# The rest of a split weight by an accumulating DMA in place of a VectorE subtraction

## Chip, core and metric

The kernel runs on one core of one Trainium2 chip. The metric is the device time of one execution in microseconds, as the median of several runs. The core has TensorE (PE in the profile, with its weight loads as PEld), VectorE (DVE), ScalarE (ACT), GpSimd (POOL) and SyncE (SP), and 16 DMA engines, which work through the queues of the engines that issue DMAs. Operands lie in SBUF, the results of matmuls in PSUM, inputs and outputs in DRAM.

## What is computed

Four layers of a diffusion backbone over 256 latent tokens and 256 context tokens, 2048 features wide. The mixers are Fourier, mLSTM in both directions, attention, and Fourier again (on the latent tokens alone).

```python
for i in range(DEPTH):                       # 4
    kind = i % N_MIXERS                      # Fourier, mLSTM, attention
    shift, scale, gate = jnp.split(sc @ ada_w[i] + ada_b[i], 3, axis=-1)
    hx = _rmsnorm(x, norm_g[i]) * (1.0 + scale[:, None]) + shift[:, None]
    # hc: the same for the context
    # kind 0: y = (fourier_mix(h) * silu(h @ w_gate)) @ w_out
    # kind 1: q, k, v, o, g, z = split(h @ w_in); y = (norm(sigmoid(o) * mlstm) * silu(z)) @ w_out
    # kind 2: q, k, v, z = split(h @ w_in);       y = (attention * silu(z)) @ w_out
    x = x + gate[:, None] * y_x
    if ctx_out:
        ctx = ctx + gate_c * y_c
return _rmsnorm(x, final_g)
```

All inputs are float32. What matters here are the products with the large weights: w_gate and w_out of both Fourier layers, w_in and w_out of the other two.

## The kernel before

A product of full precision is made from three products of the rounded type float32r. Each operand is split into a rounded part and a rest: activations h and l, weights wh and wl. TensorE adds h·wh, h·wl and l·wh in PSUM (L296 and L307).

The weights of all products are one stream of tiles of two k-tiles, [128, 2, 512], that is 512 KB each. `groups` (L250) gives the order of the matrices, 50 groups of 512 columns with 8 tiles each, so 400 tiles. One tile is called a weight step below. `make_w` (L256) makes one: a DMA on SP's queue brings it into `raw` (named wraw in the profile, 4 buffers, `WRAW`), ScalarE rounds it into `wh` (L265), VectorE subtracts that from `raw` into `wl` (L266). `wh` and `wl` have 3 buffers each (`WHL`). `next_w` (L269) hands the next pair to a product, in the order in which they are made.

`gemm` (L274) is one group: for each pair of k-tiles it takes a pair of weights and lets every accumulating bank take its three products. With 512 tokens (both streams) a weight step is 24 matmuls with 512 columns. In the attention layer's later part and in layer 3 there are the latent tokens alone, and a step is half of that.

Other work is woven into the products in pieces (`Weave`, L89): the mixers' own work, and the adaLN modulation of later layers. The latter reads its weights (`araw`, 512 KB at a time) by DMAs on SP's queue too (L175 for TensorE's variant, L198 for VectorE's), and VectorE multiplies and adds them up at L206. Along the path of TensorE also stand, for the profile's rows, the normalized operand's rest `l` (L405 in the modulation), the query and key norm (L1006), the sums of squares (L463) and the new residual `rn` (L456).

The order of TensorE's instructions is that of the program (L42). The instructions of each other engine, DMA issues on SP's and POOL's queue included, are put in order by a scheduler when the kernel is built, and each engine and each queue then works in that order, with a wait in front of an instruction whose operands or buffer are not there yet. GpSimd has little to do: in the mLSTM core it makes masks from `ub`, which a DMA brings (L779), and clears a block of `eb` (L802).

Of the kernel before, what the change touches and what calls it, by code (L numbers as in the profile page):

```python
# [21 lines left out]
# buffers of adaLN weights, weights, their parts  # L22
ARAW, WRAW, WHL = 3, 4, 3
# adaLN chunks of layer 1 on the tensor engine; pieces of woven work per piece of a product
# [3 lines left out]
# columns of the packed constants  # L28
# [17 lines left out]
def _build(tc, nc, top, A, out):  # L46
# [42 lines left out]
    class Weave:  # L89
        """Generators run in turn, each step a piece of work."""  # L90
# [35 lines left out]
    class Lazy:  # L126
        """Parts of an operand's k-tiles, made when they are first asked for."""
# [9 lines left out]
        def half(self, kt, s):  # L137
            """One stream's part."""
            self.have[kt] = self.make(kt, s, self.have.get(kt))

    def ahead(gen):
        """A product up to where all of its operand is made."""
        for what in gen:
            if what == "made":
                return gen

    def after(key, made):
        """An operand of which the last four k-tiles come from woven work."""
        def get(kt):
            if kt >= 12:  # L150
                fill.finish(key)
            return made[kt]
        return Lazy(get)
# [6 lines left out]
    def ada_finish(l, s, kts, src, nv):  # L160
        """src: the products by vector and k-tile."""
        v0 = 2 - nv
        dst = ada[:, l, s, v0:2, kts]
        V.tensor_tensor(dst, src, adab[:, l, s, v0:2, kts], ALU.add)
        if s == SC:
            V.tensor_tensor(dst, dst, ng[:, l, v0:2, kts], ALU.mult)

    def ada_pe(l, s, c, place):
        """256 columns of a layer's modulation for both vectors: on the tensor engine, k-tiles in
        turn on four column groups."""  # L170
        ps = bank()
        for kq in range(4):
            pp, tag, bufs = next(place[0])
            raw = pp.tile([P, 2, 512], F32, tag=tag, name="araw", bufs=bufs)
            Q.dma_start(raw, A["ada_p"][l, s * 8 + c, kq])  # L175
            rv = raw.rearrange("p a b -> p (a b)").rearrange("p (q n) -> p q n", q=4)
            for q in range(4):
                T.matmul(ps[32 * q:32 * q + 32, :256], cpad[:, 4 * kq + q, :], rv[:, q, :],  # L178
                         start=kq == 0, stop=kq == 3)
            yield 1  # L180
        r = ap_.tile([P, 256], F32, tag="ar", name="ar", bufs=1)
        S.copy(r, ps[:, :256])
        yield 1
        pt = bank()
        for i in range(2):
            T.transpose(pt[:, 128 * i:128 * i + 128], r[:, 128 * i:128 * i + 128], ident)
        m = ap_.tile([P, 2, 4], F32, tag="am", name="am", bufs=4)[:, :, 0:2]
        V.tensor_reduce(m, pt[:, :256].rearrange("p (i q c) -> p c i q", i=2, q=4)[:, 0:2], AX.X, ALU.add)
        ada_finish(l, s, slice(2 * c, 2 * c + 2), m, 2)
        yield 1  # L190

    def ada_dve(l, s, j, nv, row=None):
        """The same on the vector engine; with `row`, added to all partitions' rows there."""
# [32 lines left out]
    def ada_chain(chunks):  # L226
        """ada_dve in turn; each one's last part on the tensor engine comes three steps late, when
        the vector engine has it."""
# [27 lines left out]
    def make_w():  # L256
        """Two k-tiles of a group's weights, as rounded part and rest."""
# [8 lines left out]
        V.tensor_tensor(wl, raw, wh.bitcast(F32), ALU.subtract)  # L266
# [7 lines left out]
    def gemm(hl, orient, t0, t1, done, first=False, used=None, halves=False, begin=None):  # L274
        """One group of 512 weight columns, in pieces; `done(b, psum)` takes each bank.
        orient A: bank b has columns 128b.. on partitions, tokens t0..t1 free.
        orient B: bank b has tokens t0 + 128b.. on partitions, columns free.
        halves (A): each stream in banks of its own, the last k-tiles for the context first;
        done(b, psum, stream).
        begin: the first four k-tiles for the context first; begin(k) has work after its k-th."""  # L280
# [7 lines left out]
        def one(b, kt, w2, s=None):  # L288
# [7 lines left out]
            for ip, (x, w) in enumerate(((h, wh), (h, wl), (l, wh))):  # L296
# [3 lines left out]
                else:  # L300
                    lhsT, rhs, o = w[:, 128 * b:128 * b + 128], x[:, c], banks[b][:, c.start - t0:c.stop - t0]
                    # a bank's second part comes into the group that its first has begun
# [71 lines left out]
    def rstd_cols(pp, acc, tiles, name, wait=lambda: None):  # L374
        """rstd by token on partitions, [P, tiles]; acc: squares summed over all k-tiles but the last,
        and those of the last. `wait` has work for the tensor engine meanwhile."""
# [12 lines left out]
    def rstd_rows(pp, r, nt):  # L389
        """The same along the free dimension, on all partitions, in PSUM."""  # L390
# [7 lines left out]
    def modulate(l, kt, src, rows, pp, s, have):  # L398
        """hT of one k-tile and stream as parts, in `have` if those are there; src, rows: its tokens."""
# [9 lines left out]
    class Norm:  # L409
        """The norm between two layers with both streams, one after the other: the squares' sums come  # L410
        with the last product of the one, the modulation with the first of the other."""
# [24 lines left out]
    def out_proj(pp, px, l, hl, old, new_dram, c0, rates, tag="xf", bufs=5, gate=None, norm=None):  # L436
        """R = R_old + gate * (y @ W); rows of R on chip, their squares' sum, R to DRAM."""
# [3 lines left out]
        for g in range(4):  # L441
# [27 lines left out]
            if g < 3 or norm is None:  # L469
                if g == 3:  # L470
                    # the table with the square root, ahead of its use
# [18 lines left out]
    def fourier(pp, l, j, eo, F, s0):  # L490
        """eo [P, 2 (sum, difference), seqs, 512]: tokens t +- (t + 128), normed, not yet scaled by
        the modulation. F [P, 4, seqs * 256] receives the mixed group, transposed."""
# [32 lines left out]
        for par in range(2):  # L525
            for m in range(2):
                ps = bank()
                # columns: cosines of tokens 0, 2, .., 128, 1, 3, .., 127; sines of even and odd ones
# [26 lines left out]
    # =====================================================================  # L555
    # layer 0: Fourier
    # =====================================================================
    with ExitStack() as st:
# [17 lines left out]
        for l in range(4):  # L576
            # scale: norm_g * (1 + bias + product)
# [14 lines left out]
        with ExitStack() as st2:  # L592
# [3 lines left out]
            def turned(k2):  # L596
                """hT of two k-tiles, then the first product's part with the two before."""
# [70 lines left out]
    # =====================================================================  # L668
    # layer 1: mLSTM, both directions, positions in the order context, latent
    # =====================================================================  # L670
# [14 lines left out]
    with ExitStack() as st:  # L685
# [10 lines left out]
        def gates():  # L696
            """Rows of the 32 gates: input gates on partitions 0.. (forward) and 32.. (backward), forget
            gates on 64.. and 96.. ."""
# [3 lines left out]
            # k-tiles in turn on four column groups, then their sums on the rows they belong to  # L702
# [31 lines left out]
            # backward rows with each stream in its flipped order  # L734
# [33 lines left out]
        def core(c):  # L768
            """The pair's two heads, in pieces: scores (A), transposed weights (B), sums of values (C)."""
            def load(hh):  # L770
                h = 2 * c.p + hh
                ub, um = [], []
                for d in range(2):
                    u = p1.tile([P, 512], F32, tag="ub", name=f"ub{d}", bufs=2)
                    Q.dma_start(u, rows_u[d, h:h + 1, :].to_broadcast([P, 512]))
                    # the blocks on the diagonal, where a token sees a part of them
# [151 lines left out]
        def load_y(kt):  # L928
            """An earlier pair's y, once the last product has used the k-tile."""
# [41 lines left out]
    # tables with the norms' weights, and for q the scores' factor  # L971
# [10 lines left out]
    # =====================================================================  # L982
    # layer 2: attention of the latent tokens over both streams
    # =====================================================================
    pO = pool(l2st, "l2o", reuse_waits="tile", side="right")
    with ExitStack() as st:
# [8 lines left out]
        def qk_norm(ps, w, i, dst):  # L995
            """Four heads of one token tile; i: its place among the latent tokens, or None. dst gets
            them transposed, in a later piece."""
# [89 lines left out]
        def turn_y(g, o):  # L1087
            """y of the group's heads: o, times the gate, transposed and split."""
# [41 lines left out]
    with ExitStack() as st:  # L1130
# [40 lines left out]
        # =================================================================  # L1171
        # layer 3: Fourier, latent tokens
        # =================================================================
# [4 lines left out]
        with ExitStack() as st2:  # L1178
# [17 lines left out]
            def product(j):  # L1196
                """y of a group, once both of its parts are there."""
# [14 lines left out]
        for g in range(4):  # L1212
# [3 lines left out]
            def done(b, ps):  # L1216
# [15 lines left out]
                # the same with the last norm's weights  # L1232
# [16 lines left out]
# ---------------------------------------------------------------------------  # L1249
def _tiles(w):  # L1250
    """[K, N] -> [N/512, K/256, 128, 2, 512]"""
# [4 lines left out]
def _consts():  # L1256
# [21 lines left out]
    # rotary tables: cos and signed sin, [128 t, 2 token tiles, 128] each  # L1278
# [12 lines left out]
def _layout(i):  # L1291
    """Inputs in the layouts that the kernel loads."""
# [31 lines left out]
    # gates as rows: input gates of both directions, then forget gates, each on 32 partitions  # L1324
# [27 lines left out]
```

## Time and profile before

| | us |
|---|---|
| median of 3 runs | 2200.84 |
| lowest and highest run | 2197.6 and 2200.85 |
| span of the profiled execution | 2198.5 |

For the profiled execution the span is the only time; the three runs lie around it.

| Engine | busy us | share of the span |
|---|---|---|
| TensorE, matmuls | 2145.8 | 98% |
| TensorE, weight loads | 1756.6 | 80% |
| VectorE | 1547.7 | 70% |
| ScalarE | 813.5 | 37% |
| GpSimd | 17.5 | 1% |

The 16 DMA engines moved 453.15 MB, 206 GB/s over the span, and the packets of SP's queue took 59.1% of the engines' time. The mean granted clock of TensorE was 0.996.

A row of a group names line, engine and operation, what is written from what, the shape, the count, then busy time and mean ns of one, and behind the next bar the idle time of the engine just before these instructions with what ended most of it. A row of waits names the waiting instruction, what released it, the sum in us, the count and the longest. A row of the timeline begins with start and duration in us and may end with the idle time before it. A row of a stage gives its bounds and length in us, then the busy us of PE, PEld, DVE, ACT and POOL with their instruction counts, the granted clock as a share of full speed, the share of the DMA engines and GB/s. A busy engine may be one that a neighbour feeds in time: what sets the time of a stage is the wait that ends last in it.

### The profile page before, as it was taken

What the parts mean: (1) busy time and instruction counts of PE and PEld (TensorE: products, weight loads), DVE (VectorE), ACT (ScalarE), POOL (GpSimd) and SP (SyncE); (2) the same over time, 40 slices, a digit from 0 to 9 for tenths busy, and PEclk for the clock granted to TensorE, in tenths of its full rate; (3) what the DMA queues carried; (4) which work ended last, traced back from release to release, by engine and by line L of the source; (5) the groups of instructions that cost most, each with busy time, mean ns of one, the idle gap of its engine ahead of it and who ended that gap; (6) DMA issues with size and microseconds to landing.
All of it is one profiled execution on the core that took longest, in us unless ns stands there. A gap on an engine that the chain in (4) does not pass through costs nothing. (4 is left out here: it accounts for less than half of the span.)

```text
span 2198.5 us, 30359 instructions
## 1 busy us (share of the span) xinstructions
PE 2145.8 (98%) x11708; PEld 1756.6 (80%) x11708; DVE 1547.7 (70%) x2677; ACT 813.5 (37%) x1317; POOL 17.5 (1%) x29
## 2 busy tenths in 40 slices
PE   5999999999999999999999999999999999999998
PEld 2776777788788888888888888888787777999986
DVE  3542899997457876787875667655667876769986
ACT  4341232223343323332332343223336544554444
POOL 0000000000000000000000000000000000000000
PEclk9999999999999999999999999999999999999999
DMA  8866877884235564455546456663265566666774
GB/s 355 313 223 231 278 276 255 296 294 152 74 123 162 175 207 135 162 197 200 179 148 218 173 179 221 221 239 106 87 206 206 193 210 207 236 224 223 260 257 146
DMA packets 126274, 453.15 MB, mean 206 GB/s; under 512 B 14240, under 2 KB 16800, under 8 KB 123184
## 3 DMA queue, kind: packets, MB, share of 16 engines
q1 hardware_dynamic: 125840, 450.28, 59.1%
q8 instruction: 92, 1.51, 0.3%
q10 hardware_dynamic: 288, 0.92, 0.1%
q14 instruction: 54, 0.44, 0.1%
HBM read 437.48 MB, written 13.66 MB: 205 GB/s over the span
## 5 line engine op out<-in xcount | busy, mean ns | idle before, releaser
L266 DVE TENSOR_TENSOR wl<-wraw,wh 128x1024 fp32r<-128x1024 f32 x400 | 487.9, 1221 | 319.7 <-ACT wh L265 317.9
L307 PE MATMUL acc<-h,wh 128*128 128x512 f32 (+1 forms) x1936 | 696.4, 360 | 5.7 <-ACT h L404 3.9
L265 ACT CAST wh<-wraw 128x1024 fp32r<-128x1024 f32 x400 | 418.9, 1048 | 727.0 <-PE acc L307 639.4
L307 PE MATMUL acc<-l,wh 128*128 128x512 f32 (+1 forms) x1936 | 672.2, 347 | 1.8 <-DVE l L405 1.8
L307 PE MATMUL acc<-h,wl 128*128 128x512 f32 (+1 forms) x1936 | 669.8, 346 | 1.1 <-DVE wl L266 1.1
L206 DVE SCALAR_TENSOR_TENSOR aacc<-araw,cvec,aacc 128x512 f32<-128x512 f32 x780 | 552.5, 746 | 24.7 <-DMA araw<-in_ada_w_dram 20.3
L307 PE MATMUL acc<-wh,h 128*128 128x512 f32 x1024 | 428.9, 419 | 3.5 <-DVE xn L1006 2.2
L307 PEld LDWEIGHTS acc<-h,wh 128*128 128x128 f32 x1936 | 367.3, 190 | 77.2 <-issue 27.5
L307 PEld LDWEIGHTS acc<-l,wh 128*128 128x128 f32 x1936 | 366.9, 190 | 51.0 <-DVE l L405 3.4
L307 PEld LDWEIGHTS acc<-h,wl 128*128 128x128 f32 x1936 | 367.7, 190 | 44.3 <-issue 1.9
L307 PE MATMUL acc<-wh,l 128*128 128x512 f32 x1024 | 401.4, 392 | 0.5 <-DVE l L405 0.5
L307 PE MATMUL acc<-wl,h 128*128 128x512 f32 x1024 | 400.0, 391 | 0.3 <-DVE wl L266 0.3
L307 PEld LDWEIGHTS acc<-wh,h 128*128 128x128 f32 x1024 | 192.9, 188 | 52.1 <-issue 14.8
L307 PEld LDWEIGHTS acc<-wl,h 128*128 128x128 f32 x1024 | 193.2, 189 | 45.5 <-issue 7.9
L307 PEld LDWEIGHTS acc<-wh,l 128*128 128x128 f32 x1024 | 192.5, 188 | 43.3 <-DVE l L405 1.3
L178 PE MATMUL xb<-araw,cpad 128*32 128x256 f32 x896 | 74.1, 419 | 21.2 <-ACT junk L571 16.3
L216 DVE TENSOR_REDUCE am<-xb 128x4 f32<-128x512 f32 x48 | 31.4, 685 | 46.9 <-PE xb L215 46.8
L178 PEld LDWEIGHTS xb<-araw,cpad 128*32 128x32 f32 x896 | 19.9, 112 | 55.0 <-issue 20.9
L404 ACT ACTIVATE h<-mu,ada 128x256 fp32r<-128x256 f32 x80 | 37.0, 502 | 36.6 <-DVE mu L403 36.6
L462 ACT ACTIVATE sq<-rn 128x256 f32<-128x256 f32 (+1 forms) x48 | 24.7, 517 | 63.1 <-DVE rn L456 62.9
L540 PE MATMUL xb<-fU,cst 128*128 128x258 f32 (+3 forms) x320 | 47.9, 296 | 0.0
L835 PE MATMUL xb<-v,wt 128*128 128x256 f32 x192 | 46.6, 379 | 0.0
(220 smaller groups left out, 1490.9 us busy)
## 6 DMA issues: line engine op xcount, KB each, us to landing
araw<-in_ada_w_dram SPq DMA_DIRECT2D x272, 512.0 KB, 4.6
wraw<-in_w1in_dram SPq DMA_DIRECT2D x128, 512.0 KB, 3.6
araw<-in_ada_p_dram SPq DMA_DIRECT2D x112, 512.0 KB, 5.2
wraw<-in_w2in_dram SPq DMA_DIRECT2D x80, 512.0 KB, 3.5
wraw<-in_w0g_dram SPq DMA_DIRECT2D x32, 512.0 KB, 5.6
wraw<-in_w0o_dram SPq DMA_DIRECT2D x32, 512.0 KB, 4.7
wraw<-in_w1o_dram SPq DMA_DIRECT2D x32, 512.0 KB, 4.2
wraw<-in_w2o_dram SPq DMA_DIRECT2D x32, 512.0 KB, 5.1
```

Source lines behind the costliest of these rows:

```text
L178: T.matmul(ps[32 * q:32 * q + 32, :256], cpad[:, 4 * kq + q, :], rv[:, q, :], start=kq == 0, stop=kq == 3)
L206: V.scalar_tensor_tensor(accs[v], raw[:, i, :], c, accs[v], ALU.mult, ALU.add)
L216: V.tensor_reduce(m[:, v, :], pt.rearrange("p (i k) -> p i k", i=4), AX.X, ALU.add)
L265: S.copy(wh, raw)
L266: V.tensor_tensor(wl, raw, wh.bitcast(F32), ALU.subtract)
L307: T.matmul(o, lhsT, rhs, start=start, stop=stop)
L404: S.activation(h[:, c], u, AF.Identity, bias=ada[:, l, SH, s, kt:kt + 1])
L462: S.activation(sq[:, c], rn[:, b, c], AF.Square)
L540: T.matmul(ps[:, o:o + w], M[:, par, i, 128 * m:128 * m + 128], mv(i), start=i == 0, stop=i == 1)
L835: T.matmul(po[:, :256], wt[:, 128 * k:128 * k + 128], c.v[:, k, 256 * hh:256 * hh + 256], start=k == 0, stop=k == nb - 1)
```

## The change

In `make_w` the rest is no longer subtracted on VectorE. ScalarE writes the negated rounded part into `wl`, and a DMA issued on POOL's queue adds `raw` to it where it lies, so that `wl` is `raw - wh` again. `raw`, `wh` and `wl` keep their buffers and sizes, and nothing else of the program is changed; the rest of the diff takes comments out and leaves the lines where they were.

```diff
@@ make_w
         wh = wp.tile([P, 2, 512], F32R, tag="wh", name="wh", bufs=WHL)
         wl = wp.tile([P, 2, 512], F32R, tag="wl", name="wl", bufs=WHL)
         S.copy(wh, raw)
-        V.tensor_tensor(wl, raw, wh.bitcast(F32), ALU.subtract)
+        S.activation(wl, wh.bitcast(F32), AF.Copy, scale=-1.0)
+        G.dma_start(wl.bitcast(F32), raw, accum_op=ALU.add)
         made.append((wh, wl))
```

## The prediction

> **What bounds the kernel now.** I read the page's busy times first, then the groups of the edited lines, then the waits by who waited, and at last the stages.
>
> ```profile
> span 2198.5 us, 30359 instructions
> ...
> PE 2145.8 (98%) x11708; PEld 1756.6 (80%) x11708; DVE 1547.7 (70%) x2677; ACT 813.5 (37%) x1317; POOL 17.5 (1%) x29
> ```
>
> TensorE is busy for 2145.8 of 2198.5 us. All other engines together can give back at most the 52.7 us between the two, whatever is taken from them.
>
> ```profile
> L266 DVE TENSOR_TENSOR wl<-wraw,wh 128x1024 fp32r<-128x1024 f32 x400 | 487.9, 1221 | 319.7 <-ACT wh L265 317.9
> L265 ACT CAST wh<-wraw 128x1024 fp32r<-128x1024 f32 x400 | 418.9, 1048 | 727.0 <-PE acc L307 639.4
> ```
>
> The subtraction to be removed is 400 x 1221 ns = 487.9 us of VectorE. In front of it VectorE idles 319.7 us, waiting for the cast; in front of the cast ScalarE idles 639.4 us for matmuls of L307. So the cast starts when TensorE gives a buffer back: the two are early, not late. What TensorE itself waits for confirms it:
>
> ```profile
> PE acc L307 <- DVE l L405: 2.3, 4, 0.7
> PE acc L307 <- DVE xn L1006: 2.2, 1, 2.2
> PE xb L380 <- DVE sqacc L463: 2.0, 2, 1.1
> PE acc L307 <- DVE wl L266: 1.5, 3, 0.8
> PE acc L307 <- DVE rn L456: 0.9, 2, 0.5
> ```
>
> The five largest waits of TensorE's matmuls for VectorE come to 8.9 us, 1.5 of them for wl. That is all that a freer VectorE is worth on the path.
>
> **The cover in time.** ScalarE's timeline shows the rhythm of the casts, in layer 1 (first pair) and in the last product (second pair), and VectorE's the subtraction between two of the latter:
>
> ```profile
> 1207.36 1.05 ACT L265 CAST wh<-wraw 128x1024 fp32r<-128x1024 f32 x1 [4.39 <-PE acc L307]
> 1212.80 1.05 ACT L265 CAST wh<-wraw 128x1024 fp32r<-128x1024 f32 x1 [4.39 <-PE acc L307]
> ```
>
> ```profile
> 2155.04 1.05 ACT L265 CAST wh<-wraw 128x1024 fp32r<-128x1024 f32 x1 [1.67 <-PE acc L307]
> 2157.76 1.05 ACT L265 CAST wh<-wraw 128x1024 fp32r<-128x1024 f32 x1 [1.67 <-PE acc L307]
> ```
>
> ```profile
> 2156.13 1.22 DVE L266 TENSOR_TENSOR wl<-wraw,wh 128x1024 fp32r<-128x1024 f32 x1 [1.50 <-ACT wh L265]
> ```
>
> A weight step (two k-tiles) takes TensorE 5.44 us with 512 tokens and 2.72 us with 256. There are three wh/wl buffers, so from a buffer's release to its next use lie two steps: 10.9 or 5.4 us. The present refill ends 1.22 us after 2156.13, which is 2.3 us after the cast began at 2155.04: covered everywhere.
>
> **The stages.** The weight loads by matrix (issued on SP, with first and last start) cut the span, and the windows give each stage's state. The columns end in granted clock, DMA share, GB/s.
>
> ```profile
> L262 SPq DMA_DIRECT2D wraw<-in_w1in_dram x128: 327/328/424, 493.0 to 1292.0; - x128
> L262 SPq DMA_DIRECT2D wraw<-in_w2in_dram x80: 327/328/328, 1484.7 to 1843.9; - x80
> L262 SPq DMA_DIRECT2D wraw<-in_w0g_dram x32: 327/380/719, 39.0 to 290.8; - x32
> L262 SPq DMA_DIRECT2D wraw<-in_w0o_dram x32: 327/328/589, 298.6 to 486.5; - x32
> L262 SPq DMA_DIRECT2D wraw<-in_w1o_dram x32: 327/328/423, 1299.9 to 1478.9; - x32
> L262 SPq DMA_DIRECT2D wraw<-in_w2o_dram x32: 327/328/340, 1849.4 to 1953.8; - x32
> L262 SPq DMA_DIRECT2D wraw<-in_w3g_dram x32: 327/328/328, 1956.7 to 2076.2; - x32
> L262 SPq DMA_DIRECT2D wraw<-in_w3o_dram x32: 327/328/328, 2079.0 to 2172.3; - x32
> ```
>
> ```profile
> 0.00:493.00 493.00, 468.53 (x2828) 342.15 (x2829) 337.47 (x630) 152.07 (x252) 0.20 (x4) 1.00 0.78 280
> 493.00:1484.00 991.00, 987.11 (x4716) 813.09 (x4715) 679.64 (x1194) 329.06 (x545) 17.34 (x25) 1.00 0.52 176
> 1484.00:1955.00 471.00, 461.21 (x2629) 391.14 (x2628) 325.00 (x479) 221.37 (x345) 0.00 (x0) 1.00 0.54 187
> 1955.00:2180.00 225.00, 221.35 (x1508) 204.19 (x1507) 196.22 (x359) 106.37 (x168) 0.00 (x0) 0.99 0.66 225
> ```
>
> Layers 0 to 3 hold 64, 160, 112 and 64 steps. Their DMA engines are busy 0.78 x 493 = 385, 0.52 x 991 = 515, 0.54 x 471 = 254 and 0.66 x 225 = 149 us.
>
> **The change, part by part.** (1) Removed: 487.9 us of VectorE. Off the path, worth at most the 8.9 us above. (2) Added on ScalarE: 400 negations of 128x1024. The nearest row is the cast, 1048 ns for the same shape, so 419 us; ScalarE goes from 37% to about 56% busy. They stand beside TensorE's work. If that cover goes, each is 1.05 us of the refill, and evacuations of PSUM queue behind a negation that waits for its buffer, which it does no longer than the cast ahead of it. (3) Added on POOL's queue: 400 accumulating DMAs of 512 KB from SBUF to SBUF. Nothing in this trace accumulates, and no DMA is issued on POOL, so its two prices are bounded by other rows.
>
> ```profile
> 0.00:37.00 37.00, 16.18 (x126) 5.10 (x126) 12.42 (x38) 17.82 (x46) 0.20 (x4) 1.00 0.96 382
> 37.00:48.00 11.00, 9.23 (x87) 5.09 (x80) 2.86 (x11) 3.32 (x8) 0.00 (x0) 0.84 1.02 404
> ```
>
> *Engine time.* With the queues full at the start, 382 GB/s pass at 0.96 share. A move of 524 KB (512 KB) costs 524/382 = 1.37 us. From below an accumulation is one such move; nothing makes it less, since the old loads all remain. From above it is three in a row (read source, read destination, write back), 4.1 us. I take the two reads, 2.7 us, because in a load too the write runs beside the read. Added: 173, 432, 302 and 173 us in the four stages. With full engines as limit:
> - layer 0: 385 + 173 = 558 against 493: +65
> - layer 1: 515 + 432 = 947 against 991: 0
> - layer 2: 254 + 302 = 556 against 471: +85
> - layer 3: 149 + 173 = 322 against 225: +97
>
> The sum is +247 us. At 1.37 us only layer 3 is over (149 + 88 = 237, +12); at 4.1 us it is +154, +180, +242 and +186 = +762.
>
> A price that only a page states: the Trainium skill, Collectives: The Full Stack, Part 3 (on why ReduceScatter is half of AllGather), says that an addition in the DMA needs two source reads on one ring and halves about 31 GB/s per engine; my estimate from it is 2.1 us for 512 KB on 16 engines, by which the sum would be about +100 us. No row here shows an addition.
>
> *Latency.* The landing times are these:
>
> ```profile
> DMA to landing us min/median/max: 3.3/4.2/7.9
> ```
>
> ```profile
> res<-rn SPq DMA_DIRECT2D x8, 1024.0 KB, 5.7
> ...
> gate<-in_gb_dram SPq DMA_DIRECT2D x1, 1024.0 KB, 8.0
> ```
>
> A wraw load of 512 KB takes at least 3.3 us from issue to landing, a move of 1024 KB 5.7 to 8.0. The accumulation reads 1024 KB: I take 5.7 to 8.0 and keep 3.3 as the lower end; 7.9, the slowest load, with another 4.1 for crowded engines, is the upper, 12. Cast, negation and hand-overs are 2.3 us, so a refill takes 8.0 to 10.3 us. Against 10.9 us it is just hidden; against 5.4 us it isn't. The ring then sets the step at (2.72 + refill)/3 = 3.6 to 4.3 us. Layer 3 has 225/64 = 3.5 us a step now, with 2.72 in its second half, so the ring alone costs 20 to 100 us there and in layer 2's output product (32 steps in 104 us, 3.3 each). The full engines cost more in the same stages, so I add nothing for it.
>
> (4) Moved: wraw's release, from the subtraction to the landing of the accumulation.
>
> ```profile
> SPq L262 <- DVE wl L266: 971.9, 322, 14.6
> ```
>
> SP waits 971.9 us at L262 for L266. Now it waits for the landing, 5.7 us or more later than before, and the adaLN loads (L198) are queued behind it. With four buffers the cycle is landing 4.2 + 2.3 + 5.7 to 8.0, over four 3.1 to 3.6 us: below the ring of wl, so nothing more. (5) POOL's own work:
>
> ```profile
> L779 POOL TENSOR_SCALAR_AFFINE_SELECT um<-ub 128x512 f32<-128x512 f32 x16 | 15.2, 949 | 96.7 <-DMA ub<-rows_u 95.8 <-ACT eb L800 0.9
> L802 POOL MEMSET eb<- 128x128 f32 x8 | 1.6, 204 | 574.0 <-PE xb L826 388.4 <-DVE ef L819 142.0 <-ACT h L933 43.5
> ```
>
> Those 24 instructions wait in order, and so would accumulations behind them. The first group's 96 us of waits is the price if none is hidden; below, it is nothing, since layer 1 has the long steps. I take nothing and keep 96 for the range.
>
> **Forecast.** 2198.5 + 247 = 2445.5 us of span. The three runs shown (2197.6 to 2200.85) lie around the old span, their median 2.3 us above it; with that, **2448 us**.
>
> **Rivals.**
> - *Only the ring binds*: an accumulation takes the engines 2.0 us or less, and the refill of 8.0 to 10.3 us sets the short steps: +40 to +120, so 2240 to 2320, say 2280. For it: reads within SBUF may be quicker than those from DRAM. Against it: layer 3 is short of engine time at 1.4 us already. Chance 0.17.
> - *Three moves*: 4.1 us, 2960. It would turn layer 1 DMA-bound too. Chance 0.14 for 2600 and above.
> - *POOL's order*: forecast plus the 96 us, 2544. Chance 0.10.
> - *Not slower*: the accumulation lands within 5.4 - 2.3 = 3.1 us of its issue. Then all is covered, and TensorE gets back up to 8.9 us: 2192. This is decided at 3.1 us, and the fastest load of half the reads needs 3.3. Chance 0.06, half of it within 0.2%, which is about what a measurement of this kernel can tell from no change.
> - *The clock falls*: it was granted 0.84 between 37 and 48 us, after TensorE had been busy 16.18 of 37. With TensorE's busy time of layer 2 and 3 (461 and 221 us) against 556 and 322, a clock above 0.83 and 0.69 hides in the wait for the DMA. At one half it would be 922 and 442: +366 and +120, 2934 us. The stalls expected are some 1.5 us a step. The Trainium skill, TensorE: Matmul & The Clock Gate, section HAM oscillation, says that a gap above about 3.4 us halves the clock; the 0.84 agrees in direction only. Chance 0.03.
>
> The forecast itself keeps 0.50, with 2350 to 2600 as its own range. For 8 in 10 I leave out the not-slower case, the quick half of the ring's and the upper part of three moves: **2260 to 2740**. Faster 0.03, same 0.03, slower 0.94.
>
> **What the profile of the changed kernel would show.** L266 is an ACT group of 400 at about 1.05 us, VectorE falls to about 1060 us. A queue of POOL's appears with 400 DMAs; its share of the engines tells 1.37, 2.7 or 4.1 us (400 x 2.7 over the new span is 44%). In 1955 to the end the DMA share is 0.95 or more and TensorE waits at L307 for wl; a share of 0.8 with the same waits speaks for the ring. A granted clock under 0.9 in layers 2 and 3 speaks for the clock. The forecast is wrong at its root if TensorE is still 98% busy, and at its size if layer 1 takes longer than 991 us.

## The result, and the profile after

| | us |
|---|---|
| before, median of 4 runs | 2200.34 (2197.6 to 2200.85) |
| after, median of 4 runs | 2700.09 (2687.68 to 2708.81) |
| ratio | 1.2278, 95% interval 1.2254 to 1.2302 |

The change costs 500 us, twice the 247 that were forecast. The page of the changed kernel, first its span and busy times, then some groups, then the DMA queues (q1 is SP's, q0 is POOL's; the last column is the share of the 16 engines):

```profile
span 2700.7 us, 31735 instructions
...
PE 2312.1 (86%) x11708; PEld 1851.7 (69%) x11708; DVE 1096.1 (41%) x2277; ACT 1218.6 (45%) x1719; POOL 357.0 (13%) x429
...
q1 hardware_dynamic: 125840, 450.28, 46.7%
q0 software_dynamic: 57600, 209.74, 41.7%
...
L308 PE MATMUL acc<-h,wl 128*128 128x512 f32 (+1 forms) x1936 | 708.3, 366 | 177.5 <-DMA wl<-wraw 177.2
...
L308 PE MATMUL acc<-wl,h 128*128 128x512 f32 x1024 | 429.6, 420 | 139.0 <-DMA wl<-wraw 138.8
...
L266 ACT ACTIVATE wl<-wh 128x1024 fp32r<-128x1024 f32 x400 | 422.8, 1058 | 9.3
```

The negations take about what was forecast, 1058 ns each. The accumulations hold the 16 engines for 0.417 x 2700.7 / 400 = 2.82 us each; 2.7 had been taken. But TensorE now idles 388.6 us instead of 52.7, and 316 us of that are waits of its matmuls for wl, the two groups above. It is also busy for 2312.1 us with the same work, 166 more than before. The view of the cores has the reason:

```profile
core 0: 2700.7 us, clock 0.934
```

Before, the mean granted clock was 0.996. A clock of 0.934 over 2700.7 us lacks 178 us of full speed, before it lacked 9; the 169 between them match the 166 us of longer busy time. So the 502 us of span are 336 of idle time and 166 of slower matmuls.

The first loads of the matrices again give the bounds of the stages, here of layers 1 to 3, and the windows their state (the last one to the end of the span):

```profile
L262 SPq DMA_DIRECT2D wraw<-in_w1in_dram x128: 327/328/947, 576.6 to 1449.6; - x128
L262 SPq DMA_DIRECT2D wraw<-in_w2in_dram x80: 327/328/384, 1684.2 to 2150.2; - x80
...
L262 SPq DMA_DIRECT2D wraw<-in_w3g_dram x32: 327/328/328, 2332.5 to 2510.3; - x32
```

```profile
0.00:577.00 577.00, 500.62 (x2911) 362.58 (x2912) 276.58 (x582) 216.36 (x316) 53.66 (x66) 0.94 0.94 298
577.00:1684.00 1107.00, 1025.35 (x4679) 831.81 (x4678) 488.50 (x1020) 492.68 (x706) 149.39 (x184) 0.96 0.86 232
1684.00:2332.00 648.00, 518.72 (x2626) 424.70 (x2625) 199.84 (x367) 336.10 (x460) 97.21 (x113) 0.91 0.88 227
2332.00:2701.00 369.00, 267.44 (x1497) 232.64 (x1497) 131.18 (x308) 173.50 (x239) 56.76 (x66) 0.87 0.91 237
```

| us | layer 0 | layer 1 | layer 2 | layer 3 to the end |
|---|---|---|---|---|
| before | 493 | 992 | 472 | 242 |
| after | 577 | 1108 | 648 | 368 |
| added | 84 | 116 | 176 | 126 |
| forecast | 65 | 0 | 85 | 97 |
| DMA engines busy, after (share x length) | 542 | 952 | 570 | 336 |
| the same, forecast | 558 | 947 | 556 | 322 |

The last two rows show that the forecast of the engine time was right within 5% in every layer. The stages are longer than their engine time, though, layer 1 above all, where the engines are busy 0.86 of the time. What stands there can be seen at the end of a group of columns in layer 1. ScalarE's, POOL's and TensorE's timelines of the changed kernel, at one such place:

```profile
1101.98 1.05 ACT L265 CAST wh<-wraw 128x1024 fp32r<-128x1024 f32 x1 [0.76 <-PE acc L308]
1103.06 1.06 ACT L266 ACTIVATE wl<-wh 128x1024 fp32r<-128x1024 f32 x1
...
1104.50 1.04 ACT L265 CAST wh<-wraw 128x1024 fp32r<-128x1024 f32 x1
```

```profile
1104.42 0.86 POOL L267 DMA_DIRECT2D wl<-wraw  x1 [9.55 <-ACT wl L266]
1106.93 0.86 POOL L267 DMA_DIRECT2D wl<-wraw  x1 [1.65 <-ACT wl L266]
```

```profile
1108.58 0.39 PE L308 MATMUL acc<-wh,h 128*128 128x512 f32 x1
1111.51 0.80 PE L308 MATMUL acc<-wl,h 128*128 128x512 f32 x1 [2.55 <-DMA wl<-wraw]
1112.11 0.63 PE L308 MATMUL acc<-wh,l 128*128 128x512 f32 x1
1112.54 0.63 PE L308 MATMUL acc<-wh,h 128*128 128x512 f32 x1
```

Two casts stand close together, 2.5 us apart: the group's last four k-tiles are worked through bank by bank, so the last two pairs of buffers are held to the end and come free almost at once. TensorE then has little more than one step in hand (the third pair), not two. The refill lasts from 1101.98 to 1111.5, 9.5 us, 7 of them from the issue of the accumulation to its landing, when its data are in place; TensorE stalls for 2.55 us, and the matmuls behind the stall begin every 0.43 us instead of every 0.23.

### The profile page after: what moved, and what is told of

Read it like the earlier page. It is cut to its first block, busy times and chain, and to the rows that moved or that the text cites. A ratio compares the mean times of both kernels' runs of the same rounds, so it can differ in the third digit from the quotient of the medians.

```text
span 2700.7 us, 31735 instructions
## 1 busy us (share of the span) xinstructions
PE 2312.1 (86%) x11708; PEld 1851.7 (69%) x11708; DVE 1096.1 (41%) x2277; ACT 1218.6 (45%) x1719; POOL 357.0 (13%) x429
## 4 chain that ended last, share of the span: by engine, by line
PE 51%; DMA 30%; issue 14%; DVE 2%; ACT 2%; POOL 0%; POOLq 0%; SPq 0%; DVEq 0%; ACTq 0%
PE acc L308 43%; DMA wl<-wraw 25%; DMA araw<-in_ada_w_dram 2%; DMA araw<-in_ada_p_dram 2%; PE xb L178 2%; PE xb L541 1%; DVE aacc L206 1%; PE xb L836 1%; PE xb L791 1%; PE xb L508 1%; ACT wh L265 1%; PE xb L215 0%; ACT wl L266 0%; PE xb L1063 0%; PE xb L827 0%
## 5 line engine op out<-in xcount | busy, mean ns | idle before, releaser
L308 PE MATMUL acc<-h,wl 128*128 128x512 f32 (+1 forms) x1936 | 708.3, 366 | 177.5 <-DMA wl<-wraw 177.2
L308 PE MATMUL acc<-h,wh 128*128 128x512 f32 (+1 forms) x1936 | 723.4, 374 | 7.6 <-ACT h L405 2.0
L308 PE MATMUL acc<-l,wh 128*128 128x512 f32 (+1 forms) x1936 | 699.2, 361 | 1.0 <-DVE l L406 1.0
L267 POOL DMA_DIRECT2D wl<-wraw x400 | 344.7, 863 | 2241.2 <-ACT wl L266 1731.0
L308 PEld LDWEIGHTS acc<-h,wl 128*128 128x128 f32 x1936 | 392.9, 203 | 245.2 <-DMA wl<-wraw 201.9
L308 PE MATMUL acc<-wl,h 128*128 128x512 f32 x1024 | 429.6, 420 | 139.0 <-DMA wl<-wraw 138.8
L308 PEld LDWEIGHTS acc<-h,wh 128*128 128x128 f32 x1936 | 391.3, 202 | 84.1 <-issue 31.4
L266 ACT ACTIVATE wl<-wh 128x1024 fp32r<-128x1024 f32 x400 | 422.8, 1058 | 9.3
L308 PEld LDWEIGHTS acc<-l,wh 128*128 128x128 f32 x1936 | 392.2, 203 | 50.3 <-DVE l L406 1.8
L457 DVE SCALAR_TENSOR_TENSOR rn<-acc,ada,rold 128x256 f32<-128x256 f32 x80 | 35.9, 480 | 197.2 <-PE acc L308 197.1
```

The lines of the kernel that those rows point to most:

```text
L266: S.activation(wl, wh.bitcast(F32), AF.Copy, scale=-1.0)
L267: G.dma_start(wl.bitcast(F32), raw, accum_op=ALU.add)
L308: T.matmul(o, lhsT, rhs, start=start, stop=stop)
L457: V.scalar_tensor_tensor(rn[:, b, a:a + 256], ps[:, 256 * s - o:256 * s - o + 256], ada[:, l, GA, s, kt:kt + 1], ro[:, b, a:a + 256], ALU. ...
```

## The experiments

The stage lengths of the table above are used throughout. "Added" is the time less that of the kernel before on the same chip: 2194.6 us for the first four runs, 2197.2 for the next four, 2196.8 for the last four. e1 to e4, e6, e7, e11 and e12 were executed once each; the four executions of the changed kernel lie 21 us apart, so a difference of a few us between two such runs says nothing. Three theories are kept apart: A, the time that the accumulations take from the DMA engines; B, the way from a released buffer to the landed rest; C, the clock after stalls.

**The load without the wait (e1).**

```diff
-        S.activation(wl, wh.bitcast(F32), AF.Copy, scale=-1.0)
-        G.dma_start(wl.bitcast(F32), raw, accum_op=ALU.add)
+        V.tensor_tensor(wl, raw, wh.bitcast(F32), ALU.subtract)
+        G.dma_start(raw, wh.bitcast(F32), accum_op=ALU.add)
```

> The rest is again subtracted on VectorE, without the negation; beside it each step still issues an accumulating DMA of the same size on POOL, onto wraw, which nobody reads afterwards. The engines' load stays, the landing is no longer on the path to wl. Theory A (the time that 400 accumulations take from the 16 DMA engines, 2.8 us each): layers 0, 2 and 3 still have more DMA time than TensorE time, the sum of the prediction stands, 2420 to 2470 us. Theory B (the way from a released buffer to the landed rest is too long for three buffers): the stalls go, 2200 to 2270 us. Theory C (the halved clock after stalls is a large part by itself): the clock rises with the stalls' going, whatever their cause.

Measured: 2522.0 us, added 327. The stages from the windows:

```profile
0.00:573.00 573.00, 501.62 (x2984) 368.17 (x2985) 345.32 (x642) 154.39 (x256) 53.67 (x66) 0.96 0.95 298
573.00:1600.00 1027.00, 993.43 (x4657) 814.00 (x4656) 670.51 (x1183) 325.98 (x544) 152.79 (x185) 0.99 0.91 251
1600.00:2180.00 580.00, 499.61 (x2610) 413.18 (x2609) 328.07 (x480) 222.25 (x346) 96.50 (x112) 0.92 0.96 254
2180.00:2520.00 340.00, 256.42 (x1464) 222.09 (x1462) 203.78 (x373) 108.58 (x173) 56.97 (x66) 0.87 0.97 257
```

Added by layer: 80, 35, 108 and 98. The mean clock is 0.949 instead of 0.934. Two thirds of the loss are there though wl no longer waits for a landing. The time is 52 us above the upper end of A's expectation: layer 1, which has engine time to spare, loses 35, and layers 0 and 2 lose 15 to 23 us more than the forecast has. In layers 2 and 3 the engines are at 0.96 and 0.97 with a granted clock of 0.92 and 0.87: there the engines set the pace, and a full clock could not have bought more than the missing 3 to 4%.

The run does not take every landing off TensorE's path, though. The accumulation still holds wraw, as in the changed kernel, so the next load waits for it; and as its source is wh here, the next cast into that buffer waits too:

```profile
SPq L262 <- DMA wraw<-wh: 1653.1, 384, 14.5
```

```profile
ACT wh L265 <- DMA wraw<-wh: 111.2, 19, 10.3
```

The casts also wait 369 us for loads of wraw, where they waited 9 in the kernel before. So the 327 us are engine time and held buffers together. A's part is at most these 327, and the 172 us that the changed kernel costs beyond them are not all that the landings cost.

**Half the load, on the path and off it (e3, e12).** In e3 the line of the DMA is a copy:

```diff
-        G.dma_start(wl.bitcast(F32), raw, accum_op=ALU.add)
+        G.dma_start(wl.bitcast(F32), raw)
```

> The DMA on POOL copies wraw onto wl instead of adding to it: the addition is left out. Theory A: a copy takes 1.4 us of the engines, half of 2.8, so only layer 3 stays over, 2210 to 2270 us. Theory B: the landing falls only from 7.0 to about 5 us, refill about 7.3 us: the short steps and the group ends still stall, 2300 to 2420 us.

e12 is e1 with `G.dma_start(raw, wh.bitcast(F32))`.

> As e1, but with a plain copy of the same size beside the subtraction on VectorE: half the engine time (1.35 us each) and off the path. Copying overwrites wraw after its last use, the result stays. Theory A: what an accumulation costs beyond a copy is engine time, so little is left, 2205 to 2240 us, and e3's excess over this run is the wait on the path alone. If a second DMA queue by itself, or the later release of wraw, is what costs, it stays above 2350.

Measured: 2465.4 us (added 271) and 2307.7 us (added 111). POOL's queue in the pages of e1, e3 and e12, with spans of 2520.1, 2463.6 and 2305.9 us:

```profile
q0 software_dynamic: 57600, 209.74, 44.5%
```

```profile
q0 software_dynamic: 57600, 209.74, 21.9%
```

```profile
q0 software_dynamic: 57600, 209.74, 23.4%
```

Divided by 400, an accumulation takes 2.80 us of the engines and a copy 1.35, so the addition costs a second move. The four runs make a table of what is added:

| added us | wl off the path | wl on the path | difference |
|---|---|---|---|
| plain copy, 1.35 us | 111 | 271 | 160 |
| accumulation, 2.8 us | 327 | 500 | 172 |

Both expectations of A failed: a copy off the path costs 111 us and not 8 to 43, and on the path 271, which is 45 us above B's range too. e12 lies between A's range and the 2350 that was named for a second queue or a later release of wraw, so it decides neither. By layer (0 to 3) it adds 34, -4, 42 and 36, and buffers are held to the landing there as in e1. The wait of wl for the landing costs some 165 us at either load (the negations on ScalarE, below, are part of this), on top of the load's price and not in place of it. That the two sums are alike is in part chance: by layer the path adds 10, 29, 77 and 41 us with copies, and 4, 81, 68 and 28 with accumulations. Layer 1 of e3 and of e12:

```profile
537.00:1553.00 1016.00, 991.97 (x4693) 812.40 (x4692) 491.53 (x1027) 493.26 (x706) 96.41 (x184) 1.00 0.71 253
```

```profile
526.00:1514.00 988.00, 981.57 (x4663) 808.04 (x4663) 674.52 (x1188) 327.44 (x543) 100.76 (x185) 1.00 0.74 261
```

There the path costs 29 us with copies (1017 against 988) and 81 with accumulations (1108 against 1027). The landing fits that direction: 7.0 us for an accumulation and 4.9 for a copy, as the tile's views of the changed kernel and of e3 have it:

```profile
DMA to landing us min/median/max: 4.5/7.0/12.6
```

```profile
DMA to landing us min/median/max: 2.8/4.9/9.7
```

**The negation alone (e2), and with another order at the group's end (e10).** `V.tensor_tensor(wl, wl.bitcast(F32), raw, ALU.add)` stands in place of the DMA; e10 adds the order of e4 below.

> ScalarE negates as in the change, VectorE adds wraw in place of the DMA. All theories: 2195 to 2210 us. If ScalarE's 400 negations (423 us) cost anything on the path, it shows here as the excess over 2200.

> e2 (negation on ScalarE, addition on VectorE, no DMA added) with the order of e4 in the last four k-tiles. Theory B: e2's 33 us come from the group ends, where cast, negation and addition of two steps follow one upon the other after a common release; without the common release 2200 to 2212 us. Rival (the negations hold up ScalarE's other work everywhere): 2225 us or more.

Measured: 2227.9 us (added 33), and 2224.9 us, ratio 1.0127 with an interval from 1.0097 to 1.0156 (added 28). So the negations are not free, against all theories: some 20 to 30 of the 172 us are theirs. The kernel before with the same order (e8, below) is 8 us longer than without it, so with that order the negations cost 20 us and not 33. B's 2200 to 2212 failed, then, and the rival's 2225 was met (2224.9), but up to 13 of the 33 us may still lie at the group ends. In e2 TensorE's matmuls wait 18.4 us for wl, 15 times, instead of 1.5:

```profile
PE acc L308 <- DVE wl L267: 18.4, 15, 3.0
```

Where the rest of the 33 us lies was not followed further.

**No common release at the group's end (e4), and its control (e8).**

```diff
         for b in range(nb):
-            for kt in range(12, 16):
-                one(b, kt, wa if kt < 14 else wb)
-                if kt == 13:
-                    yield
+            one(b, 12, wa)
+            one(b, 13, wa)
+            yield
+        for b in range(nb):
+            one(b, 14, wb)
+            one(b, 15, wb)
             done(b, banks[b][:, :n])
             yield
```

> The changed kernel, but the last four k-tiles of a group are worked through weight pair by weight pair, not bank by bank, so that the last but one pair of buffers is released one step earlier and no two come free at once. Theory A: nothing, 2670 to 2710 us. Theory B: layer 1 loses most of its stalls (about 4 us in each of 20 groups) and their clock, layer 2 some: 2550 to 2630 us.

> The kernel before, subtraction on VectorE, with the order of e4 in the last four k-tiles. Theory B: TensorE waits for wl only 1.5 us there, so nothing to win, 2185 to 2205 us; evacuations of all banks come closer together, which may cost a few us. It is the control of e4, whose gain would then be the accumulation's and not the order's.

Measured: 2591.7 us, 108 less than the changed kernel, with layer 1 at 1068 instead of 1108 and layer 2 at 612 instead of 648. In the kernel before the same order costs 8 us (2205.1 us, ratio 1.0035, interval 1.0023 to 1.0048). So the gain is that of the earlier release, as B has it, and A's "nothing" falls. Most of layer 1's stalls do not go, though: TensorE's waits for wl there fall from 72.6 us (34 waits) to 48.5 (25). The common release makes a third of them; what makes the others was not followed, but the slowest landing, 12.6 us, is longer than two steps.

**A fourth pair of buffers (e6, e7), and with the order of e4 (e11).** `WHL` is 4 in e6 and 3 in e7. In both, room is made alike:

```diff
-ARAW, WRAW, WHL = 3, 4, 3
+ARAW, WRAW, WHL = 2, 4, 4
...
-    ada = cp.tile([P, 4, 3, 2, KT], F32, name="ada")
+    ada = adab
...
-        return p1.tile([P, 512], F32, tag="w2", name=name, bufs=5)
+        return p1.tile([P, 512], F32, tag="w2", name=name, bufs=4)
...
-        return p2.tile([P, 512], F32, tag="w2", name=name, bufs=7)
+        return p2.tile([P, 512], F32, tag="w2", name=name, bufs=6)
...
-                    sq = pp.tile([P, n], F32, tag="ys", name="sq", bufs=2)
+                    sq = pp.tile([P, n], F32, tag="ys", name="sq", bufs=1)
```

> Four wh and wl buffers in place of three; for their room two adaLN buffers in place of three, the modulation in place, and one buffer fewer of the mixers' and the squares' scratch (the next run has all of these but the fourth buffer). Theory A alone: within 30 us of the next run. Theory B: three steps instead of two to cover a refill, so layer 1 falls from 1108 to about 1030 us and layer 2 by 60 us; in all 120 to 200 us below the next run.

> The control of the run before: the same smaller buffers, with three wh and wl. All theories: 2690 to 2740 us, since VectorE's adaLN work is off the path.

> Four wh and wl buffers (as e6) and the order of e4 together. Theory B: the remaining waits on the path shrink until the engines' time is left, which e1 gave as 2522 us; 2540 to 2590 us. If A and B overlap fully, the order adds nothing to the fourth buffer: 2620 to 2640 us.

Measured: 2631.7 us with four pairs, 2771.9 with three, so the fourth is worth 140 us. The smaller buffers cost 72 against the changed kernel, which no theory had; 45 of them are in layer 0. Layers 1 and 2, of e6 and then of e7:

```profile
617.00:1682.00 1065.00, 1012.47 (x4724) 826.90 (x4723) 500.57 (x1040) 493.27 (x707) 151.65 (x185) 0.98 0.89 244
1682.00:2278.00 596.00, 501.11 (x2638) 416.08 (x2637) 199.41 (x367) 332.81 (x459) 96.49 (x113) 0.93 0.95 247
```

```profile
622.00:1740.00 1118.00, 1026.18 (x4708) 831.85 (x4707) 496.65 (x1032) 494.08 (x707) 150.54 (x185) 0.97 0.86 231
1740.00:2405.00 665.00, 522.16 (x2620) 430.94 (x2618) 199.96 (x367) 335.43 (x460) 97.40 (x114) 0.89 0.86 222
```

With the same load, 53 and 69 us go where a refill has one step more to land in, and TensorE's waits for wl in layer 1 fall from 70.9 us to 7.0. That is the clearest sign that the way from release to landing sets the time there. Layer 1 stays 35 us above the 1030 expected all the same. Both measures together give 2594.8 us, 5 above the upper end of what was expected: the order adds 37 us to the fourth pair, so the two overlap in part.

**The clock (e5, e9).** Zero products keep TensorE at work where it would wait.

```diff
                 T.matmul(o, lhsT, rhs, start=start, stop=stop)
+                if ip == 0 and w2 is not keep["last"]:
+                    keep["last"] = w2
+                    for _ in range(keep["n"] * 512 // rhs.shape[-1]):
+                        T.matmul(o, zero, rhs, start=False, stop=False)
```

> The changed kernel; in layer 3 alone, in each weight step, TensorE adds a zero product five times (512 columns, 0.23 us each, 1.1 us a step, 64 steps, +73 us of work) between the first matmul with wh and the first with wl, where it otherwise waits idle. Theory C (a stall costs a second time, by the halved clock in the window behind it): the granted clock of layer 3 rises from 0.87 to 0.95 or more and the stage, 368 us from its first load to the end, gets shorter in spite of the work, by 15 to 40 us. Rival, the prediction's own step (the clock hides in the wait for the DMA, whose engines are at 0.94 there): the clock may rise, the stage stays within 8 us or gets longer.

> The changed kernel; in layer 1 alone, once in each group of columns, in its second weight step, where the refill that started at the group's end is late, TensorE adds a zero product ten times (2.3 us, some 19 groups, +43 us of work) before its first matmul with wl. The load on the DMA engines is the same. Theory C (the halved clock is time lost in layer 1, where the engines are at 0.86 and TensorE still sets much of the pace): the clock of layer 1 rises from 0.96 to 0.99, and the stage falls from 1107 to 1065 to 1090 us in spite of the work. Rival (the clock costs nothing by itself, the DMA's lateness sets the stage): 1100 to 1150 us.

Measured: 2721.4 us (ratio 1.2387, interval 1.2362 to 1.2412) and 2699.2 us (ratio 1.2285, interval 1.2191 to 1.2380). Layer 3 of e5 and layer 1 of e9:

```profile
2329.00:2719.00 390.00, 348.80 (x2257) 316.53 (x2257) 132.24 (x308) 178.25 (x240) 57.03 (x66) 0.96 0.87 225
```

```profile
572.00:1678.00 1106.00, 1050.81 (x4893) 855.35 (x4893) 488.73 (x1021) 493.74 (x707) 150.14 (x185) 0.98 0.86 232
```

The clock rose in both, from 0.87 to 0.96 and from 0.96 to 0.98. Layer 3 got 21 us longer with 73 us of added work, layer 1 stayed (1106 against 1107) with 43. In both the rival's range held, and C's shorter stage is not seen in either. C isn't refuted for layer 1: idle time there fell by only 26 us, from 82 to 55, so some 17 of the 43 us of added work were made good by faster matmuls. What a stall costs through the clock, beyond what the refill behind it would have waited anyway, stays open.

## Why the prediction was off by a factor of two

- **What bounds the kernel**: right as far as the runs show. VectorE went from 1547.7 to 1096.1 us busy, and no gain from that shows in any run.
- **Engine time, 2.7 us by two reads**: right, 2.82, and the engine time of all four layers within 5%. That the write runs beside the read, the reason given for it, no run tested alone. The Trainium skill, Collectives: The Full Stack, Part 3, has the second read, and the ratio of 2.80 to 1.35 agrees; its rate does not. By it the estimate was 2.1 us, and a copy of 512 KB in 1.35 us is 24 GB/s per engine, not 31. The measurement decides.
- **A stage as the larger of engine time and TensorE time**: too small. By it the forecast had 247 us for the load alone; with wl off the path the runs show 327, and with half the load 111 where the same sum gives 12. Whether the 80 to 100 us between come from engine time and TensorE time that do not pack, or from the buffers that e1 and e12 still hold to the landing, is open.
- **Latency, "The full engines cost more in the same stages, so I add nothing for it"**: this is the step that failed. The runs show the wait on the path as a term of its own, 172 us on top of e1's 327 (160 on top of 111 with copies), of which the negations have 20 to 30. By layer the difference to e1 is 68 and 28 us in layers 2 and 3, together 96. The prediction had 20 to 100 for the ring in the short steps there, so the term that it left out was of about the right size. The largest part is in layer 1, 81 us, which the prediction had at nothing by "Against 10.9 us it is just hidden".
- **Two steps of cover from release to next use**: wrong at each group's end, where two pairs come free together. The views of the kernel before show it: at 1228.68 and 1230.53, in ScalarE's timeline, two casts stand 1.9 us apart instead of 5.4. This is a part only: without the common release (e4) a third of the waits for wl in layer 1 goes.

```profile
1228.68 1.06 ACT L265 CAST wh<-wraw 128x1024 fp32r<-128x1024 f32 x1 [0.77 <-PE acc L307]
1230.53 1.05 ACT L265 CAST wh<-wraw 128x1024 fp32r<-128x1024 f32 x1
```

- **Landing 5.7 to 8.0 us**: right in the median, 7.0, but the slowest took 12.6. The refill was mostly of the right size; its cover was not.
- **Negations at nothing**: 33 us (e2), 20 with the other order (e10 against e8).
- **The later release of wraw at nothing**: doubtful, and not tested alone. In e1, where the rest does not wait for the landing, TensorE's matmuls wait 42.0 us for the cast, which needs wraw, and a buffer of wh that the DMA holds there; whether full engines or the later release delays it was not separated. A run with more wraw buffers would have told.

```profile
PE acc L308 <- ACT wh L265: 42.0, 23, 6.8
```

- **POOL's order, up to 96 us**: no sign of it. In the changed kernel `um` waits 57.3 us for `ub`, less than the 95.8 before, and the waits of `eb` fell to some 20 us. No run tested it alone.
- **The clock falls, chance 0.03**: it fell, to 0.87 to 0.96 by stage, and TensorE is busy 166 us longer. That its cost hides behind full engines holds in e1's layers 2 and 3 as far as their shares of 0.96 and 0.97 go; for the rest it is open.
- **The range 2260 to 2740**: 2700 lies in it, but by luck. Its upper part was there for three moves of 4.1 us each, which did not come (2.82). The forecast's own 2350 to 2600 does not hold it, and the prediction's sign for a wrong size, layer 1 longer than 991 us, came true with 1108.

## What to carry to other kernels

Work moved to a DMA can be paid twice: in the time of the DMA engines, and in the landing that stands between a buffer's release and its next use. Here the second came on top of the first, so neither may be dropped because the other is larger. When an experiment takes the landing off one buffer's path, look which other buffers the DMA still holds. Count the cover of a ring of buffers at the place where the fewest steps lie between release and use (here the end of a group, where two come free at once), not in its steady rhythm; two casts side by side in the old timeline were the sign. And an engine at 70% beside one at 98% gave nothing when a part of its work was taken away.

## What the runs showed of the hardware

An accumulating DMA of 512 KB within SBUF takes 2.8 us of the 16 engines and lands in 7.0 us (median, 4.5 at least); a copy takes 1.35 and lands in 4.9. Short stalls can lower TensorE's clock. Behind the wait of 2.55 us shown above the granted clock was 0.50, and the matmuls ran at about half their rate until about 1114.2, some 3 us; the first row is a stage that begins where the wait ends:

```profile
1111.50:1114.20 2.70, 2.69 (x6) 2.15 (x7) 2.63 (x4) 0.00 (x0) 0.56 (x1) 0.50 1.03 225
```

```profile
1114.24 0.50 PE L308 MATMUL acc<-wl,h 128*128 128x512 f32 x1
1114.59 0.40 PE L308 MATMUL acc<-wh,l 128*128 128x512 f32 x1
```

The Trainium skill, TensorE: Matmul & The Clock Gate, section HAM oscillation, puts the limit at gaps above about 3.4 us; the row here has a shorter one, and the row decides. Over layer 1 of the changed kernel, the clock in the 2 us behind a wait of TensorE was lower than before it after each of the 11 waits of 2.8 us or more (0.50 to 0.83), after 5 of the 8 between 1.9 and 2.6, and after none of the 15 between 0.5 and 1.7 that began at full clock.
